# Constant rows and memory tokens made during attention, and first-stage buffers in another order, in a hybrid decoder layer

## The chip, the cores and the metric

The kernel runs on one core of a Trainium2 chip. The metric is the device time of one execution in microseconds (us), as a median over several runs. The engines are TensorE (PE, matrix products and transposes), VectorE (DVE), ScalarE (ACT), GpSimd (POOL) and SyncE (SP), which issues the transfers (DMAs). Each engine works through its own list of instructions in order and waits where an operand or a buffer is not ready yet.

## The reference, cut to what matters

One layer of a decoder on 1024 tokens of width 1024, all in float32. In the first sub-layer one input projection gives q, k, v of an attention, z, x, B, C and dt of a Mamba-2 mixer (SSD) and two gates; the second attends to 256 memory tokens; the third is a feed-forward.

```python
h = rms_norm(x, g_pre_mix[l])
q, k, v, z, xbc, dt_raw, ga, gs = _split(h @ w_in[l], IN_SIZES)
o_att = stick_breaking_attention(q, k, v)          # 16 heads
o_ssm = ssd_branch(z, xbc, dt_raw, ...)            # 32 heads in 4 groups, chunks of 128 tokens
merged = sigmoid(ga) * (o_att @ w_br_att[l]) + sigmoid(gs) * (o_ssm @ w_br_ssm[l])
x = x + rms_norm(merged @ w_mix_out[l], g_post_mix[l])
h = rms_norm(x, g_pre_xa[l])
mem_n = rms_norm(mem, g_mem[l])                    # 256 x 1024
x = x + rms_norm(memory_cross_attention(h, mem_n, w_xq[l], w_xkv[l], w_xo[l]), g_post_xa[l])
h = rms_norm(x, g_pre_ffn[l])
x = x + rms_norm(swiglu(h, w_gu[l], w_down[l]), g_post_ffn[l])
```

The mixer's decay between two tokens of a chunk is exp(a_cs[t] − a_cs[s]) for s ≤ t, and zero above the diagonal.

## The kernel before

Every float32 matrix is split into a high and a low part of a reduced format (`hi_sb`, an ACT copy on L96 or a POOL one on L92; `lo_of`, a subtraction on L99), and every product is three matmuls (L102 to L104, L213 to L215, L453 to L455). An operand must therefore be loaded, split on ACT, then on DVE, before PE can use it.

The work runs in stages. Each stage opens pools of SBUF and PSUM buffers and closes them at its end; a pool of a later stage is laid over the addresses of closed ones, and a new tile waits for the last reader of each old tile that it covers. So the order in which pools are opened decides who waits for whom. Inside a stage the build's scheduler sets the order of the instructions on every engine from its own timeline, and the code adds a few fixed orders: `behind(marks)` places what it holds after the given instructions.

1. First stage. x is loaded, normalised with the gain `g_pre_mix` (with `junk` as scratch) and transposed. The products with w_in are made in seven block products in place of eight (Strassen's way), for which sums and differences of the blocks of h and of the weights are needed: `hb` holds b11, b21, b22, t1 and later t2, t3, t4, each as high and low part (h and l at the end of the name). Here v's first products (`pv`, weights split into `vh` and `vl` of the pool vsplit) and dt (`pdt`) are made.
2. Second stage (L419 on). `rest_of_v` makes v's remaining products and then z. It begins with `s1 = a21 + a22` of weights (tile `zo`, L463), two differences (L466, L467), splits of these into `zh` and `zl` (L96, L99), and the product `mb`. t3 and t4 come back from `tc_d` in DRAM and are split.
3. Convolutions of x, B and C, dt's chain, the early gates.
4. Attention. `dense` projects q and k for two heads at a time in two PSUM buffers `mm`; the evacuation (L786 to L797) writes `qs`, `kh` and, through `gt`, `kl`, and SyncE copies halves between them. `va` and `vb` are loaded, added and split by POOL. Then scores (`sc`), a running sum on DVE (L845), transposes (`tr`), weights `wth` and `wtl`, and values (`av`); the last gates (`gt`, from `g_proj`'s dense) run between them.
5. SSD, mixed with the memory's K and V projection. The exponents of the decays are made by PE: `colrows` times `keyrows` (L1032) sums, for each pair of tokens, rows loaded from `sum_d` and `key_d` into constant patterns. These patterns are built at the stage's start (L964 to L981: POOL's selects, DVE's casts). `open_four` loads B and C of four chunks (`bfm`, `cfm`, `btm`), `prep` x (`xs`). `memory(m)` loads 128 memory tokens, normalises and transposes them and splits them into `mh` and `mlo` (tiles oth and otl).
6. The branches' outputs, the mix, cross-attention and the feed-forward.

Of the kernel before, what the change touches and what calls it, by code (L numbers as in the profile page):

```python
# [34 lines left out]
def hybrid_block(ctx, tc, a, out, dbg=None):  # L35
# [41 lines left out]
    tc_d = [scr(f"tc_d{i}", [P, 4, HALF]) for i in range(2)]  # L77
    kT_d = scr("kT_d", [P, KT, ML])
# [161 lines left out]

    HB = ("b11", "b21", "b22", "t1")
    HT = ("t2", "t3", "t4")
    LATE_GATES = 4
    with ExitStack() as pa:
# [22 lines left out]
        with ExitStack() as p1:  # L267
            t4 = pool(p1, "t4x0", 4)
            tt = pool(p1, "tcomb", 6)
            bt = pool(p1, "b12t", 3)  # L270
            vh = pool(p1, "vsplit", 8)
            mp = pool(p1, "memp")
            mt4 = pool(p1, "t4mem", 2)
# [9 lines left out]
            gx = load_gain(mp, "g_pre_mix")  # L283
# [30 lines left out]
            def normed(c, eng):  # L314
                xt = xts[c]
                junk = mk(mt4, [P, D], BF16, "junk")
# [82 lines left out]
            d11, d0, d1 = [mk(mt4, [64, HALF], F32, "du", bufs=3) for _ in range(3)]  # L399
# [320 lines left out]
        with ExitStack() as p2:  # L720
# [84 lines left out]

            def gate_proj(gi):
                def ev(ps, half):
                    gt = mk(t2, [P, HALF], F32, "gt")
                    A.activation(gt, ps, AF.Sigmoid)
# [95 lines left out]
            for q in qk_quanta(0):  # L905
                for f in q:
                    f()
            NM = 2 * NH
# [15 lines left out]


# [8 lines left out]
    with ExitStack() as p3:  # L934
        AHEAD = 2
        gb = pool(p3, "gbs", 2)
# [3 lines left out]
        ep = pool(p3, "exps", 1)  # L940
# [15 lines left out]

        NROW, HEADS, ONES, PAIRS, LARGE = 2, 32, 0, 64, 2.0 ** 127
# [5 lines left out]
        before, within = mk(t4, [P, GH, P], F32, "s4"), mk(t4, [P, GH, P], F32, "s4")  # L968
        G.memset(before, 1.0)
        G.affine_select(before, before, [[0, GH], [-1, P]], ALU.is_gt, 0.0, base=-2 * PAIRS, channel_multiplier=2)  # L970
        within = within[:, 0:4]
        G.memset(within, -(2.0 ** 120))
        G.affine_select(within, within, [[0, 4], [1, P]], ALU.is_ge, 0.0, base=2 * PAIRS, channel_multiplier=-2)
        G.affine_select(within, within, [[0, 4], [-1, P]], ALU.is_ge, 0.0, base=1 - 2 * PAIRS, channel_multiplier=2)
        hr = slice(HEADS, HEADS + 2 * GH)
        for t in colrows:
            V.tensor_copy(t, before)
            V.tensor_tensor(t[hr], *[ident[hr, HEADS + j * GH:HEADS + (j + 1) * GH].unsqueeze(2).to_broadcast([2 * GH, GH, P]) for j in range(2)], ALU.add)
        for t in keyrows:
            V.tensor_copy(t.rearrange("p (c s) -> p c s", s=P), within)  # L980
            V.tensor_scalar(t[ONES:ONES + 2], low[ONES:ONES + 2, 0:1].to_broadcast([2, HALF]), 0.0, 1.0, ALU.mult, ALU.add)  # L981
# [84 lines left out]
        def outp(n):  # L1066
# [30 lines left out]
        def flip(n):  # L1097
# [8 lines left out]
            for k in range(4):  # L1106
                T.transpose(pt[:, k, :], y[:, k * P:(k + 1) * P], ident)
# [41 lines left out]
        gj = mk(wp, [P, 4, D], F32, "bw")  # L1149
        gm, junk_m = gj[:, 0], gj[:, 1]  # L1150
        marks = []

        def memory(m):
            xt = mk(wr, [P, D], F32, "wraw")
            nc.sync.dma_start(xt, a["mem"][0][m * P:(m + 1) * P, :])
            ms = mk(stats, [P, 1], F32, "ms")
            A.activation(junk_m, xt, AF.Square, scale=D ** -0.5, accum_out=ms)
            V.scalar_tensor_tensor(xt, xt, rstd_of(ms), gm, ALU.mult, ALU.mult)
            for kh in range(2):
# [695 lines left out]
```

## Time and profile before

| what | value |
|---|---|
| median of 3 runs | 2599.42 us (2596.26 to 2602.25) |
| the profiled execution | 2601.74 us, its span 2600.0 us |
| PE busy | 2494.5 us, 96% of the span |
| DVE, ACT, POOL busy | 69%, 44%, 33% |
| HBM read and written | 199.84 MB and 74.19 MB |

The span is what the profile covers; the run's own time is 1.74 us longer. PE's share is high nearly all the way: in the page's 40 slices of 65 us only the first shows less than 80%. Waits of PE are thus short and lie at the joints of stages. In rows of a timeline the first number is the start, the second the busy time, "xN" the count of instructions drawn together, and the bracket the idle time of the engine just before and what ended it.

### The profile page before, as it was taken

Reading aid. Unit: us, or ns where it says so; the run is one execution under the profiler, and the core shown is the slowest. Engines: PE = TensorE matmul, PEld = TensorE weight load, DVE = VectorE, ACT = ScalarE, POOL = GpSimd, SP = SyncE. Lnnn points to the kernel's source line nnn. Section 1 sums busy time; section 2 is a strip of 40 time slices with the busy share of each in tenths; the row PEclk is TensorE's granted clock in tenths of the full one; section 3 lists DMA queues with packets and bytes.
Section 4 is the critical chain, followed back from the end, with each engine's and each line's share of the span. In section 5 each row is a group of like instructions: output and inputs, shape, how many; then the busy total and the mean of one; then the engine's idle time right before and its main releaser. Section 6 shows DMA issues by size and latency. Waiting matters only on the chain. (4 is left out here: it accounts for less than half of the span.)

```text
span 2600.0 us, 32345 instructions
## 1 busy us (share of the span) xinstructions
PE 2494.5 (96%) x11866; PEld 2061.7 (79%) x11866; DVE 1805.3 (69%) x2091; ACT 1135.6 (44%) x2023; POOL 849.8 (33%) x652
## 2 busy tenths in 40 slices
PE   6999999999999999989999999999999999999998
PEld 5788787787887878877888788887787888887877
DVE  6656868767587887587788665415459666665997
ACT  5233455555455665555544312314333333334343
POOL 3221543443111211254555150101114323323662
PEclk9999999999999999999999999999999999999999
DMA  7331432332543434355332472311232232224232
GB/s 252 136 98 56 147 130 87 114 106 89 155 102 101 110 102 106 90 177 186 108 93 70 143 251 85 121 58 49 82 117 73 77 97 74 85 94 162 98 130 97
DMA packets 254983, 292.92 MB, mean 113 GB/s; under 512 B 16991, under 2 KB 175208, under 8 KB 254698
## 3 DMA queue, kind: packets, MB, share of 16 engines
q1 hardware_dynamic: 254826, 290.87, 35.7%
q8 instruction: 93, 1.52, 0.2%
q14 instruction: 64, 0.52, 0.1%
HBM read 199.84 MB, written 74.19 MB: 105 GB/s over the span
## 5 line engine op out<-in xcount | busy, mean ns | idle before, releaser
L845 DVE TENSOR_TENSOR_SCAN n<-n,mask 128x128 f32<-128x128 f32 (+7 forms) x128 | 188.6, 1499 | 23.5 <-ACT n L844 22.2
L99 DVE TENSOR_TENSOR sw<-sf,sw 128x512 fp32r<-128x512 f32 x150 | 131.0, 885 | 66.5 <-ACT sw L96 66.2
L181 POOL TENSOR_TENSOR sf<-wr,wr 128x512 f32<-128x512 f32 x38 | 59.1, 1554 | 275.9 <-DMA wr<-in_w_gu_dram 139.9
L862 ACT ACTIVATE wth<-tr,mone 128x512 fp32r<-128x512 f32 x192 | 110.4, 584 | 83.2 <-PE tr L859 82.3
L96 ACT ACTIVATE sw<-sf 128x512 fp32r<-128x512 f32 x150 | 91.9, 627 | 110.8 <-PE mm L215 94.1
L863 DVE SCALAR_TENSOR_TENSOR wtl<-tr,wth 128x512 fp32r<-128x512 f32 x192 | 99.7, 544 | 51.5 <-ACT wth L862 51.4
L96 ACT ACTIVATE sw<-wr 128x512 fp32r<-128x512 f32 x113 | 71.0, 629 | 128.9 <-PE mm L215 128.7
L102 PE MATMUL mm<-oth,bw 128*128 128x512 f32 (+1 forms) x320 | 122.6, 383 | 4.7 <-DVE a L1144 2.4
L215 PE MATMUL mm<-h,sw 128*128 128x512 f32 x320 | 125.0, 392 | 1.8 <-DVE sw L99 1.8
L213 PE MATMUL mm<-h,sw 128*128 128x512 f32 x320 | 123.0, 392 | 2.9 <-ACT h L96 2.3
L214 PE MATMUL mm<-h,sw 128*128 128x512 f32 x320 | 125.3, 392 | 0.0
L104 PE MATMUL mm<-oth,bw 128*128 128x512 f32 (+1 forms) x320 | 119.5, 374 | 1.4 <-DVE bw L99 1.4
L99 DVE TENSOR_TENSOR sw<-wr,sw 128x512 fp32r<-128x512 f32 x113 | 102.1, 904 | 25.8 <-ACT sw L96 17.8
L103 PE MATMUL mm<-otl,bw 128*128 128x512 f32 (+1 forms) x320 | 119.0, 372 | 0.0
L598 DVE SCALAR_TENSOR_TENSOR b<-b,prmT,b 128x1023 f32<-128x1023 f32 (+2 forms) x72 | 106.1, 1474 | 12.1 <-ACT b L596 11.5
L92 POOL TENSOR_SCALAR v<-va 128x512 fp32r<-128x512 f32 x16 | 20.6, 1287 | 286.4 <-PE av L872 166.7
L844 ACT ACTIVATE n<-sc 128x512 f32<-128x512 f32 (+1 forms) x192 | 88.5, 493 | 45.7 <-PE tr L859 28.9
L150 POOL TENSOR_SCALAR rstd<-ms 128x1 f32<-128x1 f32 x74 | 27.5, 372 | 231.2 <-ACT x L1366 111.0
L102 PE MATMUL p<-bw,h 128*128 128x512 f32 x256 | 99.0, 392 | 3.3 <-DVE x L1368 2.4
L104 PE MATMUL p<-bw,h 128*128 128x512 f32 x256 | 100.2, 392 | 0.0
L103 PE MATMUL p<-bw,h 128*128 128x512 f32 x256 | 99.9, 390 | 0.0
L183 POOL TENSOR_TENSOR sf<-wr 128x512 f32<-128x512 f32 x38 | 62.4, 1641 | 112.1 <-DVE sw L99 112.1
(608 smaller groups left out, 8069.6 us busy)
## 6 DMA issues: line engine op xcount, KB each, us to landing
wr<-in_w_gu_dram SPq DMA_DIRECT2D x80, 256.0 KB
wr<-in_w_in_dram SPq DMA_DIRECT2D x36, 512.0 KB
zr<-in_w_in_dram SPq DMA_DIRECT2D x28, 512.0 KB
gu_d<-t SPq DMA_DIRECT2D x44, 256.0 KB
wraw<-in_w_in_dram SPq DMA_DIRECT2D x20, 512.0 KB
zs_d<-zo SPq DMA_DIRECT2D x32, 256.0 KB
xs_d<-b SPq DMA_DIRECT2D x32, 256.0 KB
kl<-gt SPq DMA_DIRECT2D x64, 128.0 KB
```

Source lines behind the costliest of these rows:

```text
L96: A.activation(o, i, AF.Copy)
L99: eng.tensor_tensor(o, i, hi.bitcast(F32), ALU.subtract)
L102: first = T.matmul(ps, sh, mh, start=start, stop=False)
L103: T.matmul(ps, sh, ml, start=False, stop=False)
L104: T.matmul(ps, sl, mh, start=False, stop=stop)
L213: T.matmul(ps, w[0][:, k, :], bh, start=first and k == 0, stop=False, skip_group_check=True)
L214: T.matmul(ps, w[0][:, k, :], bl, start=False, stop=False, skip_group_check=True)
L215: T.matmul(ps, w[1][:, k, :], bh, start=False, stop=last and k == 3, skip_group_check=True)
L598: V.scalar_tensor_tensor(acc[:, sh:], y[:, :S - sh], cw(3 - sh, f), acc[:, sh:], ALU.mult, ALU.add)
L845: V.tensor_tensor_scan(nt[:, 0:L][:, ::-1], nt[:, 0:L][:, ::-1], mask[:, S - L:][:, ::-1], 1.0, ALU.mult, ALU.max)
L862: A.activation(wh[:, t0 * P:], pt[:, t0 * P:], AF.Identity, bias=mone)
L863: V.scalar_tensor_tensor(wl[:, t0 * P:], pt[:, t0 * P:], -1.0, wh[:, t0 * P:].bitcast(F32), ALU.add, ALU.subtract)
```

## The change

Five edits, which the diff shows:

- `patterns()` and `memory()` run in the attention stage, behind the first and the second part of the first two heads' q and k projection. The patterns are made once and stored to DRAM (`colpat_d`, `keypat_d`); the two tiles of memory tokens are normalised, transposed, split and stored to `mem_d`. The SSD stage loads them: colrows twice, keyrows twice, mh and mlo in two halves each.
- The pool `ep`, which holds low, colrows and keyrows, is opened first in the SSD stage, and so lies over other old tiles (b22 and its neighbours) than before.
- A small activation `warm` behind the last gate brings in the exponential's table.
- `flip(n)`'s transposes are placed behind the last diagonal matmul of chunk n + 2.
- The first stage's pools are opened in another order, two of them new (`dtu` for the tiles du, `gain`), one renamed (`sqs`, the junk).

```diff
+    colpat_d = scr("colpat_d", [P, S])
+    keypat_d = scr("keypat_d", [P, HALF])
+    mem_d = [scr(f"mem_d{i}", [P, KT, ML]) for i in range(2)]
...
         with ExitStack() as p1:
+            vh = pool(p1, "vsplit", 8)
+            bt = pool(p1, "b12t", 3)
+            dp = pool(p1, "dtu", 3)
+            mp = pool(p1, "memp")
+            gp = pool(p1, "gain")
+            jp = pool(p1, "sqs", 2)
             t4 = pool(p1, "t4x0", 4)
             tt = pool(p1, "tcomb", 6)
-            bt = pool(p1, "b12t", 3)
-            vh = pool(p1, "vsplit", 8)
-            mp = pool(p1, "memp")
-            mt4 = pool(p1, "t4mem", 2)
...
+                    gated.append(A.activation(gt, ps, AF.Sigmoid))
...
+            def patterns():
+                col, row, t = [mk(bp, [P, S], F32, "n1") for _ in range(3)]
+                before = t.rearrange("p (h s) -> p h s", s=P)
+                G.memset(before, 1.0)
+                G.affine_select(before, before, [[0, GH], [-1, P]], ALU.is_gt, 0.0, base=-2 * PAIRS, channel_multiplier=2)
+                V.tensor_copy(col.bitcast(F32R), t)
...
+                V.tensor_tensor(col[hr].rearrange("p (h s) -> p h s", s=P).bitcast(F32R), *heads, ALU.add)
+                nc.sync.dma_start(colpat_d, col)
...
+            def memory():
+                gm = mk(bp, [P, S], F32, "n1")
+                junk = mk(bp, [P, HALF], F32, "n0").bitcast(BF16)
+                nc.sync.dma_start(gm, a["g_mem"][0].partition_broadcast(P))
+                for m in range(2):
+                    xt = mk(bp, [P, S], F32, "n1")
+                    nc.sync.dma_start(xt, a["mem"][0][m * P:(m + 1) * P, :])
+                    ms = mk(stats, [P, 1], F32, "ms")
+                    A.activation(junk, xt, AF.Square, scale=D ** -0.5, accum_out=ms)
+                    V.scalar_tensor_tensor(xt, xt, rstd_of(ms), gm, ALU.mult, ALU.mult)
+                    for kh in range(2):
+                        pt = mk(pst, [P, HALF], F32, "tr")
+                        for k in range(4):
+                            T.transpose(pt[:, k * P:(k + 1) * P], xt[:, (kh * 4 + k) * P:(kh * 4 + k + 1) * P], ident)
+                        hi, lo = [mk(wt, [P, HALF], F32R, "wt" + n) for n in "hl"]
+                        A.activation(hi, pt, AF.Copy)
+                        V.tensor_tensor(lo, pt, hi.bitcast(F32), ALU.subtract)
+                        for d, t in zip(mem_d, (hi, lo)):
+                            nc.sync.dma_start(d[:, kh * 4:kh * 4 + 4, m * P:(m + 1) * P], t.bitcast(F32).rearrange("p (k t) -> p k t", t=P))
+
+            for n, q in enumerate(qk_quanta(0)):
                 for f in q:
                     f()
+                if n == 0:
+                    patterns()
+                if n == 1:
+                    memory()
...
+            with behind(gated[-1:]):
+                A.activation(warm, mone, AF.Exp)
...
+        ep = pool(p3, "exps", 1)
         gb = pool(p3, "gbs", 2)
...
-        ep = pool(p3, "exps", 1)
...
         for t in colrows:
-            V.tensor_copy(t, before)
-            V.tensor_tensor(t[hr], *[ident[hr, HEADS + j * GH:HEADS + (j + 1) * GH].unsqueeze(2).to_broadcast([2 * GH, GH, P]) for j in range(2)], ALU.add)
+            nc.sync.dma_start(t.rearrange("p h s -> p (h s)").bitcast(F32), colpat_d)
         for t in keyrows:
-            V.tensor_copy(t.rearrange("p (c s) -> p c s", s=P), within)
-            V.tensor_scalar(t[ONES:ONES + 2], low[ONES:ONES + 2, 0:1].to_broadcast([2, HALF]), 0.0, 1.0, ALU.mult, ALU.add)
+            nc.sync.dma_start(t.bitcast(F32), keypat_d)
...
+            d["last"] = ins
...
-            for k in range(4):
-                T.transpose(pt[:, k, :], y[:, k * P:(k + 1) * P], ident)
+            with behind([chk[n + 2]["last"]] if n + 2 in chk else []):
+                for k in range(4):
+                    T.transpose(pt[:, k, :], y[:, k * P:(k + 1) * P], ident)
...
-        with behind(chk[AHEAD - 1]["issued"]):
-            nc.sync.dma_start(gm, a["g_mem"][0].partition_broadcast(P))
-            for m in range(2):
-                memory(m)
+        for kh in range(2):
+            for t, src in zip((mh, mlo), mem_d):
+                nc.sync.dma_start(t[:, kh * 4:kh * 4 + 4].bitcast(F32), src[:, kh * 4:kh * 4 + 4])
```

How the instructions stand at three places, before and after. First DVE at the joint of the first and second stage (tc are block combinations of h, b22 and t2 its split blocks, zr weights, zo their sum). Before:

```order
L345 TENSOR_TENSOR tc_501<-tr_494,b_122_505 128x512
L337 TENSOR_TENSOR b22l_119<-tr_494,b22h_118 128x4x128
L348 TENSOR_TENSOR tc_500<-tr_494,tc_499 128x512
L350 TENSOR_TENSOR tc_502<-tr_484,tc_500 128x512
L337 TENSOR_TENSOR t2l_126<-tc_500,t2h_125 128x4x128
L463 TENSOR_TENSOR zo_660<-zr_371,zr_375 128x1024
L463 TENSOR_TENSOR zo_661<-zr_373,zr_377 128x1024
L466 TENSOR_TENSOR zr_371<-zr_622,zr_371 128x1024
L407 TENSOR_TENSOR du_582<-du_580,pv_602 64x512
L466 TENSOR_TENSOR zr_373<-zr_624,zr_373 128x1024
```

And after, in the same place:

```order
L359 TENSOR_TENSOR tc_511<-tr_504,b_122_515 128x512
L477 TENSOR_TENSOR zo_672<-zr_381,zr_385 128x1024
L477 TENSOR_TENSOR zo_673<-zr_383,zr_387 128x1024
L351 TENSOR_TENSOR b22l_123<-tr_504,b22h_122 128x4x128
L362 TENSOR_TENSOR tc_510<-tr_504,tc_509 128x512
L480 TENSOR_TENSOR zr_381<-zr_632,zr_381 128x1024
L480 TENSOR_TENSOR zr_383<-zr_634,zr_383 128x1024
L364 TENSOR_TENSOR tc_512<-tr_494,tc_510 128x512
L351 TENSOR_TENSOR t2l_130<-tc_510,t2h_129 128x4x128
L481 TENSOR_TENSOR zr_632<-zo_672,zr_632 128x1024
L481 TENSOR_TENSOR zr_634<-zo_673,zr_634 128x1024
L103 TENSOR_TENSOR zl_681<-zo_672,zh_680 128x512
```

The sums of weights (before L463, now L477) moved ahead of b22l and of t2l; the differences follow between them. The tile zo lies at the addresses of vl before, and of g_pre_mix and junk now.

Next DVE while q and k of the first heads are projected (mm is the projection's PSUM tile, wlo the next weights' low part, the n_ tiles those of patterns and memory). Before, behind the first evacuation of q, it reads:

```order
L788 TENSOR_TENSOR gt_5296<-mm_5269,qs_5294 128x512
L99 TENSOR_TENSOR wlo_5416<-wraw_5413,whi_5415 128x1024
L788 TENSOR_TENSOR gt_5327<-mm_5302,qs_5294 128x512
L797 TENSOR_TENSOR gt_5368<-mm_5339,kh_5364 128x512
L99 TENSOR_TENSOR wlo_5601<-wraw_5598,whi_5600 128x1024
```

After:

```order
L802 TENSOR_TENSOR gt_5308<-mm_5281,qs_5306 128x512
L927 CAST n_871_5314<-n_873_5316 128x1024
L930 TENSOR_TENSOR n_871_5314<-ident_91 16x1024
L103 TENSOR_TENSOR wlo_5505<-wraw_5502,whi_5504 128x1024
L802 TENSOR_TENSOR gt_5353<-mm_5328,qs_5306 128x512
L936 CAST n_872_5315<-n_872_5315 128x512
L937 TENSOR_SCALAR n_872_5315<-ident_91 2x512
L950 SCALAR_TENSOR_TENSOR n_881_5368<-n_881_5368,rstd_5372,n_879_5365 128x1024
L811 TENSOR_TENSOR gt_5457<-mm_5428,kh_5453 128x512
```

The pattern's cast and addition stand in front of the weights' split and the second q half, the memory's first norm in front of the first k half.

Last, SyncE at the SSD's start (g_d is a late gate's store, o_d attention's output). Before:

```order
L991 DMA bfm_9976<-bf_d 128x512
L993 DMA cfm_9978<-cf_d 128x512
L810 DMA g_d<-gt_9900 128x512
L995 DMA btm_9980<-bt_d_64 128x4x128
L995 DMA btm_10392<-bt_d_64 128x4x128
L877 DMA o_d_70<-oT_9893 64x512
L877 DMA o_d_71<-oT_9893 64x512
L989 DMA keyrows_2051_9954<-key_d 8x512 x2
L1025 DMA colrows_2049_9952<-sum_d 1x8x128 x2
L1025 DMA colrows_2050_9953<-sum_d 1x8x128 x2
L1239 DMA bw_9973<-in_g_mem_dram 128x1024
L1155 DMA wraw_10034<-in_mem_dram 128x1024
```

After:

```order
L1025 DMA colrows_2072_10042<-colpat_d 128x1024
L1025 DMA colrows_2073_10043<-colpat_d 128x1024
L826 DMA g_d<-gt_9989 128x512
L1027 DMA keyrows_2074_10044<-keypat_d 128x512
L1027 DMA keyrows_2075_10045<-keypat_d 128x512
L1037 DMA bfm_10054<-bf_d 128x512
L1039 DMA cfm_10056<-cf_d 128x512
L1041 DMA btm_10058<-bt_d_64 128x4x128
L1071 DMA colrows_2072_10042<-sum_d 1x8x128 x2
L1071 DMA colrows_2073_10043<-sum_d 1x8x128
L1035 DMA keyrows_2074_10044<-key_d 8x512
```

Four loads of patterns stand ahead of bfm, cfm and btm, and the rows of sum_d and key_d are written into the loaded tiles; the loads of xs, which stood before all of these, now come behind them.

More of the change, by code (lines that the diff above doesn't have):

```diff
@@ L1148, in hybrid_block @@
         mlo = mk(ot, [P, KT, ML], F32R, "otl")
-        gj = mk(wp, [P, 4, D], F32, "bw")
-        gm, junk_m = gj[:, 0], gj[:, 1]
         marks = []
[L1153 to L1159, printed above, removed]
-                pt = mk(ps, [P, 4, P], F32, "mm", bufs=2)
-                for k in range(4):
-                    T.transpose(pt[:, k, :], xt[:, (kh * 4 + k) * P:(kh * 4 + k + 1) * P], ident)
-                ks, cs = slice(kh * 4, kh * 4 + 4), slice(m * P, (m + 1) * P)
-                A.activation(mh[:, ks, cs], pt, AF.Copy)
-                V.tensor_tensor(mlo[:, ks, cs], pt, mh[:, ks, cs].bitcast(F32), ALU.subtract)
         def mem_quanta():
```

28 lines of the change are left out of this document (14 added, 14 removed).

## The prediction

> **What bounds the kernel now.** I read the page's first two parts, then the windows around the three places that the change touches, then the timelines of single engines inside them.
>
> ```profile
> span 2600.0 us, 32345 instructions
> PE 2494.5 (96%) x11866; PEld 2061.7 (79%) x11866; DVE 1805.3 (69%) x2091; ACT 1135.6 (44%) x2023; POOL 849.8 (33%) x652
> ```
>
> PE is busy for 2494.5 of 2600.0 us, so at most 105.5 us can be won by removing its waits, plus whatever its clock loses. A change that leaves the matrix work alone, as this one nearly does, is worth what it does to those 105 us. The windows (columns: stretch, length, then busy time and count of PE, weight load, DVE, ACT, POOL; granted clock, DMA share, GB/s) say where some of them lie:
>
> ```profile
> 56.00:58.00 2.00, 1.97 (x9) 0.91 (x7) 2.00 (x2) 0.60 (x1) 0.00 (x0) 1.00 0.17 67
> 58.00:64.00 6.00, 0.00 (x0) 0.00 (x0) 5.87 (x7) 1.70 (x4) 2.09 (x2) 0.71 0.56 141
> 64.00:76.00 12.00, 9.05 (x24) 6.71 (x25) 12.00 (x14) 7.52 (x14) 4.42 (x2) 0.57 0.56 183
> 76.00:100.00 24.00, 24.00 (x108) 19.87 (x107) 11.05 (x18) 4.42 (x7) 0.00 (x0) 1.00 0.41 126
> 660.00:680.00 20.00, 20.00 (x90) 16.57 (x89) 3.30 (x4) 6.57 (x10) 8.50 (x6) 1.00 0.82 242
> 680.00:700.00 20.00, 19.54 (x96) 15.89 (x95) 11.98 (x14) 10.57 (x21) 1.06 (x1) 1.00 0.49 124
> 1100.00:1140.00 40.00, 27.22 (x136) 19.75 (x135) 37.83 (x47) 26.08 (x45) 17.14 (x15) 0.91 0.57 174
> 1140.00:1240.00 100.00, 92.78 (x556) 80.17 (x555) 74.29 (x82) 55.83 (x101) 47.84 (x45) 0.98 0.56 175
> ```
>
> Three different situations. At 58 to 64 PE does nothing at all, and from 64 to 76 it runs 24 matmuls in 12 us, while right after it runs 108 in 24 us: this is where the first stage hands over to the second. At 660 to 700, where attention's first q and k are projected, PE has 0.46 us of idle time in 40, and DVE and ACT are mostly free. At 1100 to 1140, where the SSD starts, PE idles 12.8 us and DVE is busy 37.83 of 40: DVE bounds that stretch. From 1140 on PE loses another 7.2 us in 100.
>
> **The hand-over at 58 us (first-stage pools in another order).** The rows, DVE and SyncE first, then PE:
>
> ```profile
> 40.92 0.94 SPq L260 DMA_DIRECT2D zr<-in_w_in_dram  x1
> 44.69 0.69 DVE L345 TENSOR_TENSOR tc<-tr,b 128x512 f32<-128x512 f32 x1 [0.33 <-PE tr L325]
> 46.32 0.69 DVE L337 TENSOR_TENSOR b22l<-tr,b22h 128x512 fp32r<-128x512 f32 x1 [0.94 <-ACT b22h L336]
> 48.31 0.69 DVE L337 TENSOR_TENSOR t2l<-tc,t2h 128x512 fp32r<-128x512 f32 x1
> 55.94 2.36 DVE L463 TENSOR_TENSOR zo<-zr,zr 128x1024 f32<-128x1024 f32 x2 [6.94 <-PE pv L214]
> 58.22 1.22 DVE L466 TENSOR_TENSOR zr<-zr,zr 128x1024 f32<-128x1024 f32 x1
> 59.95 1.21 DVE L466 TENSOR_TENSOR zr<-zr,zr 128x1024 f32<-128x1024 f32 x1
> 61.09 2.34 DVE L467 TENSOR_TENSOR zr<-zo,zr 128x1024 f32<-128x1024 f32 x2
> 66.13 4.64 DVE L99 TENSOR_TENSOR zl<-zo,zh 128x512 fp32r<-128x512 f32 x4
> 57.58 0.39 PE L396 MATMUL pdt<-b21l,wds 128*64 128x512 f32 x1
> 64.10 2.08 PE L453 MATMUL mb<-zh,t1h 128*128 128x512 f32 x4 [6.13 <-ACT zh L96]
> 69.02 0.80 PE L454 MATMUL mb<-zl,t1h 128*128 128x512 f32 x1 [2.85 <-DVE zl L99]
> ```
>
> The next product needs zh and zl, the halves of zo, the sum of L463. DVE is free from 49.0 us (48.31 + 0.69), but L463 does not start until 55.94: its operands are weights, and what releases it is a PE matmul of the old product pv. That is a wait for memory, not for data: zo lies where vl lay, which the last v matmuls read. Then everything queues on DVE, ACT splits at 64, PE gets its first four matmuls at 64.10 and the next at 69.02. With the pools in the other order zo, zh and zl lie over the gain row, the junk of the norm and the x tiles, last read by the first stage's transposes, the last of which releases L345; the order has L463 right behind L345. So from 45.4: two L463 to 47.7, b22l to 48.4, one combination (0.69) to 49.1, two L466 (2.4) to 51.5, a combination and t2l (1.4) to 52.9, L467 to 55.3, four zl at about 0.65 each, as the short ones of this form are here, from 55.3 to 57.9. PE finishes its last pdt at 58.0, starts with the four zh matmuls, and by then has all its zl. The cover for the DVE sums is thus PE's own work to 58 us, with nothing to spare at the end but nothing missing either; b22l and t2l come 1.4 and 4 us later than before.
>
> The price: 24 matmuls of this kind take 24 x 24.00/108 = 5.3 us in the next window; now they take the 18 us from 58 to 76. That is 12.7 us. I take 12.5, since the first zl may be late by a few tenths. Upper end 13; lower end 8, if the weights a11, whose load is issued at 40.92, arrive some us late for L466 and push the zl back. The half-clock belongs to this sum: the granted clock is 0.71 and 0.57 in the two windows and 1.00 on both sides, so it goes with the gap. The Trainium skill, "TensorE: Matmul & The Clock Gate", Part 1 (the HAM clock gate), says the clock halves after an idle window of about 3.4 us and returns after about as much sustained work. The trace agrees in kind: the gap is 6 us, and by that rule a leftover gap below 3.4 us would cost only itself.
>
> What is late next: the t3 and t4 splits are not needed until the later products, and PE then runs without a gap for 24 us. The first-stage sums stand ahead of them, not behind.
>
> **The SSD start (rows and tokens loaded instead of made).**
>
> ```profile
> 1086.01 2.36 POOL L970 TENSOR_SCALAR_AFFINE_SELECT s<-s 128x1024 f32<-128x1024 f32 x1
> 1090.67 1.45 DVE L99 TENSOR_TENSOR s2r<-s,s2r 128x512 fp32r<-128x512 f32 x1 [2.15 <-ACT s2r L96]
> 1097.67 0.42 SPq L993 DMA_DIRECT2D cfm<-cf_d  x1
> 1101.79 0.63 ACT L96 ACTIVATE ch<-cfm 128x512 fp32r<-128x512 f32 x1 [2.01 <-DMA cfm<-cf_d]
> 1104.65 1.29 DVE L977 CAST colrows<-s 128x1024 fp32r<-128x1024 f32 x2
> 1105.85 0.76 DVE L980 CAST keyrows<-s 128x512 fp32r<-128x512 f32 x2
> 1106.64 2.35 DVE L978 TENSOR_TENSOR colrows<-ident 16x1024 fp32r<-16x1024 f32 x2
> 1110.56 0.70 PE L1032 MATMUL dec<-colrows,keyrows 128*128 128x512 f32 x2 [0.36 <-DMA colrows<-sum_d]
> 1131.41 1.43 PE L1162 MATMUL mm<-ident,wraw 128*128 128x128 f32 x8 [3.32 <-DVE otl L1165]
> L1158 DVE SCALAR_TENSOR_TENSOR wraw<-wraw,rstd,bw 128x1024 f32<-128x1024 f32 x2 | 3.6, 1776 | 0.2 <-POOL rstd L151 0.2
> L1165 DVE TENSOR_TENSOR otl<-mm,oth 128x512 fp32r<-128x512 f32 x3 | 2.0, 677 | 0.0
> ```
>
> Removed from DVE: 1.29 + 0.76 + 2.35 + 3.6 + 2.0 = 10.0 us of the 37.83, all where DVE is the bound; with them go PE's wait of 3.32 us for otl and its 16 transposes. Given back: in the new order the s2r splits that stood ahead (1090.67 is one) come into this stretch, some 2 to 3 us. The warm table load adds nothing in sum; it only moves up.
>
> What replaces it is DMA, ordered by memory again: colrows and keyrows now lie over b22, which the last late-gate matmuls read, so their loads are issued at about 1097, with cfm. They are 1.5 MB, with bfm, cfm and btm 2.3 MB; the window moves 174 GB/s at a share of 0.57, so 305 GB/s full, 7.5 us: landed about 1105. Then sum_d's rows are written into colrows, a second DMA in series. cfm shows what a lone one takes, 1097.67 to 1101.79, 4.1 us; so the first exponent matmul comes at 1109 to 1110, against 1110.56 now. Nothing is gained up to there; the gain comes after it, from the lighter DVE, at most 10 us less the 2.5 given back. The memory halves are another 2 MB (6.6 us at that rate) in the queue with the first weights, and PE's projection of K could use them from about 1117. I take 4 us, half of 7.5, since xs and weights share the queue with 2 MB that were not there. Ends: +10 and −3. The Trainium skill, "DMA: Bandwidth & Descriptors", Anatomy of one DMA, gives about 2.0 us fixed a DMA, most of it the receipt of the last write, and would speak against a copy through DRAM followed by a dependent write. By its figures the series takes an estimated 5.2 us plus the queue, no worse than mine, and the 4.1 us of cfm contain it.
>
> **The projection of q and k (patterns and memory added).** Here the change adds work where PE has no slack:
>
> ```profile
> 658.24 1.03 PE L588 MATMUL tr<-ident,b 128*128 128x128 f32 x8
> 659.09 0.50 PE L102 MATMUL mm<-b11h,whi 128*128 128x512 f32 x1
> 664.53 2.40 POOL L822 TENSOR_TENSOR va<-va,vb 128x1024 f32<-128x1024 f32 x1 [6.57 <-DMA vb<-v_d]
> 672.39 0.69 DVE L788 TENSOR_TENSOR gt<-mm,qs 128x512 fp32r<-128x512 f32 x1
> 675.74 0.60 ACT L795 ACTIVATE kh<-mm 128x512 fp32r<-128x512 f32 x1 [3.38 <-PE mm L104]
> 678.92 3.30 SPq L779 DMA_DIRECT2D kl<-gt  x4
> 683.70 0.56 PE L842 MATMUL sc<-kh,qs 128*128 128x128 f32 x3
> ```
>
> Sixteen transposes at 1.03/8 cost 2.1 us by their busy time, 1.7 us by the pace at which eight of them pass (658.24 to 659.09): I take 1.7 lost in full, since PE is busy 20.00 of 20. The DVE work is half of 1.29, 0.76 and 2.35 (one copy of each now), the norms' 3.6 and four differences at 0.677: 8.5 us; DVE has 24.7 us free in these 40, so it costs nothing by its sum. These steps cost by their place in the queues. POOL: a memset and a select (the 2.36 of L970) behind va at 664.53 and in front of the v splits. DVE: the cast waits for POOL, and the split of the next weights and gt (before at 672.39) are queued behind it. ACT: the Square of memory tile 0 stands in front of kh's evacuation (before at 675.74) and waits for a load, whose buffer is the one that the cast reads; k's second half needs kh's PSUM buffer. SyncE: the store of the pattern waits for DVE, and memory tile 0 waits for its buffer; the q copies, two weight loads and keypat are behind them; the kl copies come 1 to 2 us later. PE's first scores at 683.70 are the consumer. The walk: va ends at 666.9, memset, select and a gap put the pattern at about 671.5; the cast ends at 672.2, the load, at cfm's 4.1 us, at 676.3, so the Square ends near 677.5 and kh comes 1.5 to 3 us later; two PSUM buffers cover most. Between 0 and 5 us of stall, I take 1: the row it is nearest to is the window's 0.46 us of idle. If that cover is gone (a load landing 5 us later than I think), every us of it is one of PE.
>
> Flip's transposes behind a later pd move four short matmuls on PE, 0 ± 1 us.
>
> **Sum.** 12.5 + 4 − 1.7 − 1 = 13.8 us. From the profiled execution (span 2600.0, run 2601.74) that is about 2588; from the median of 2599.42 it is 2585.6. A measurement of this kernel tells 0.2%, 5.2 us, from no change.
>
> **Rivals.**
>
> 1. The SSD start gains nothing, or attention stalls by its full 5 us: DMA takes DVE's place as bound. For it: DMA is at 0.57 on average there and about 3.5 MB come into 20 us. Against: PE waited mostly for DVE, not DMA. Gain 12.5 + 0 − 1.7 and − 1 to − 5, so 6 to 10: 2590 to 2594, with the −3 2597. Chance 0.18.
> 2. The SSD start recovers nearly all, +10, and attention hides everything: 12.7 + 10 − 1.7 = 21, 2578. For it: 20 us of idle to win there. Against: the loads start no earlier than 1097. Chance 0.13.
> 3. The gap at 58 us is only renamed: L463 goes early, but L466 or zl waits for something else (the a11 load, or a PSUM bank), so DVE finishes where it did. For it: the chain on DVE has no slack at 57.9. Against: DVE idle 6.94 us in the row above, with its data there. Gain about 2: 2595 to 2600. Chance 0.06.
> 4. Slower. The added steps block attention's queues: ACT's Square stands in order in front of kh, and kh in front of all scores. If memory tile 0 lands at 676 it costs 1 us; each us later is one. It decides against the change only when it eats 13.8 and 5.2 more beyond that 1 us, a landing at 695. For it: the load waits for the cast, the cast for POOL, POOL for va, and the DMA share of 0.82 at 660 to 680 is the highest window here. Against: va ends at 666.9, memset and select take under 4 us, and 512 KB at 242 GB/s take 2.2 us. Time 2605 to 2615. Chance 0.05.
>
> **How the numbers follow.** The forecast itself (2580 to 2590) has 0.58. Faster by over 0.2% is below 2594.2: forecast, rival 2 and most of rival 1, 0.58 + 0.13 + 0.16 = 0.87. Within 0.2%: rival 3 and the rest of rival 1, 0.08. Slower 0.05. The range runs from below rival 2, with the scatter of the median (±3), to rival 1's middle: 2575 to 2594.
>
> **What would show it.** In the new trace: L463's successor starts near 45.5 without a wait for PE; the windows 58 to 76 have the clock 1.00 and PE full; zl's first use waits under 1 us. At 660 to 690 there are 16 more transposes, and PE waits under 2 us for kh or PSUM. At the SSD start the first exponent matmul comes at the same distance from the last value matmul, DVE is busy 27 to 31 of 40 us, and no wait of 3 us for otl. I am wrong if the gap of 58 us reappears under another releaser, if PE shows a wait of over 5 us in the q and k projection, or if exponent matmuls wait for colrows by more than 3 us.

## The result and the profile after

The changed kernel takes 2596.68 us, the median of 12 runs (2594.89 to 2607.05), against 2598.78 us for the kernel before, beside it (12 runs). The ratio is 0.9994, with a 95% interval of 0.9985 to 1.0003: no change that can be told. The forecast was 2585.6 us with a range of 2575 to 2594, so it was wrong, by some 11 us. The profiled execution spans 2594.7 us, against 2600.0; the profiled run of before lay some 2 to 3 us above its own median, and the medians differ by 2.1 us, which the interval doesn't tell from nothing.

The windows of the changed kernel, asked for the same stretches (columns as in the prediction), and one more at 640:

```profile
58.00:64.00 6.00, 6.00 (x29) 4.92 (x28) 2.03 (x4) 0.59 (x1) 6.00 (x3) 1.00 0.32 80
64.00:76.00 12.00, 12.00 (x54) 9.76 (x53) 5.39 (x9) 5.88 (x11) 0.50 (x2) 1.00 0.67 215
640.00:660.00 20.00, 16.77 (x70) 13.31 (x70) 2.93 (x5) 7.02 (x10) 6.43 (x5) 0.91 0.54 170
660.00:680.00 20.00, 17.10 (x80) 13.62 (x78) 8.78 (x8) 5.63 (x9) 10.84 (x11) 1.00 0.95 265
680.00:700.00 20.00, 19.51 (x94) 16.29 (x94) 17.25 (x19) 13.09 (x29) 1.82 (x3) 0.91 0.77 217
1100.00:1140.00 40.00, 33.14 (x188) 27.43 (x187) 26.41 (x32) 21.49 (x37) 15.92 (x13) 0.87 0.89 278
1140.00:1240.00 100.00, 91.67 (x534) 78.25 (x534) 84.98 (x92) 59.35 (x108) 55.08 (x50) 1.00 0.55 175
```

The gap at 58 us is gone, as forecast: PE is full and its clock is 1.00. From 640 to 700 PE now lacks 6.6 of 60 us, at a DMA share that went to 0.95; before it lacked 3.4 (two of its windows are in the prediction, this is the third):

```profile
640.00:660.00 20.00, 17.03 (x80) 13.69 (x81) 13.37 (x12) 8.61 (x14) 7.01 (x4) 1.00 0.44 128
```

At the SSD's start PE does 33 us of work in 40 where it did 27.

So the expected gain was made and then lost again. Where, is seen by following PE's lead: for every matmul that both kernels have, its start in the trace of before less its start in the other trace; the table gives the median over the 20 us of the time of before that begin at the number in its head. A positive number is time won up to there. The first column is behind the hand-over, 600 ahead of the convolutions' end, 660 at q's first matmuls, 740 behind the first heads, 1080 at attention's end, 1260 and 1440 inside the SSD, 2560 near the end.

| kernel | 120 | 600 | 660 | 740 | 1080 | 1260 | 1440 | 2560 | median us, ratio to before |
|---|---|---|---|---|---|---|---|---|---|
| changed kernel | 11.7 | 13.6 | 8.9 | −0.1 | 1.3 | 8.8 | 5.2 | 5.5 | 2596.68, 0.9994 (0.9985 to 1.0003) |
| pools_only | 12.3 | 13.4 | 8.6 | 8.6 | 8.6 | 3.8 | 3.2 | 5.5 | 2598.98, 1.0000 (0.9989 to 1.0011) |
| all_but_pools | 0.9 | 2.7 | 2.8 | −3.5 | −2.7 | 0.9 | 0.8 | −1.6 | 2604.59, 1.0017 (1.0007 to 1.0028) |
| pools_tail_pinned | 11.7 | 13.3 | 12.7 | 12.6 | 11.9 | 5.3 | 5.3 | 8.8 | 2594.63, 0.9983 (0.9974 to 0.9993) |
| square_behind_k | 11.2 | 13.2 | 9.2 | 0.4 | 2.7 | 6.6 | 5.3 | 6.8 | 2597.71, 0.9990 (0.9980 to 1.0000) |
| patterns_only | 11.5 | 13.2 | 8.4 | 5.2 | 7.0 | 2.2 | 1.9 | 4.7 | 2598.07, 0.9995 (0.9985 to 1.0004) |
| memory_only | 8.3 | 8.3 | 2.3 | −4.9 | −3.7 | −1.7 | −2.4 | −3.1 | 2601.75, 1.0001 (0.9992 to 1.0011) |
| flip_free | 12.0 | 13.8 | 7.9 | 0.9 | 3.8 | 6.7 | 6.1 | 9.2 | 2596.25, 0.9993 (0.9982 to 1.0004) |
| spread_and_pinned | 11.4 | 11.1 | 10.6 | 11.0 | −7.4 | −3.7 | −6.8 | −7.1 | 2609.19, 1.0037 (1.0024 to 1.0051) |
| pools_tail_flip | 9.5 | 11.4 | 9.3 | 9.1 | 9.6 | 6.2 | 6.1 | 6.0 | 2592.42, 0.9972 (0.9962 to 0.9981) |
| all_tail_pinned | 11.8 | 13.2 | 12.7 | 5.6 | 7.0 | 11.5 | 11.1 | 11.2 | 2590.75, 0.9970 (0.9961 to 0.9980) |
| all_tail_flip_early | 11.8 | 13.4 | 12.9 | 7.1 | 8.1 | 12.6 | 12.3 | 13.1 | 2594.02, 0.9976 (0.9966 to 0.9986) |
| traffic_alone | 11.0 | 12.6 | 12.0 | 9.5 | 10.5 | 10.4 | 10.4 | 9.9 | 2591.68, 0.9971 (0.9961 to 0.9982) |

Each lead is of one execution, counted against the one profile of before, and single executions of one kernel differ by up to 13.7 us in all (flip_free, 2592.55 to 2606.22). A step of the lead inside one row is read more safely than its end, but it scatters too. Up to 1080 us the changed kernel and flip_free have the same order of instructions on every engine and of the transfers (by line, tile name and shape), and from 660 to 740 they lose 9.0 and 7.0 us. From 1085 to 1255 the changed kernel and all_tail_pinned have the same orders, and from 1080 to 1260 they win 7.5 and 4.5 us. So a difference of 2 to 3 us between two steps is not told from scatter. The medians come from 5 to 12 runs, each ratio from runs of both kernels on the same chip.

In the first row there are three losses: 4.8 us between 600 and 660, 9.0 between 660 and 740, 3.6 behind 1260. The first two in the rows of the changed kernel, PE, DVE and ACT:

```profile
644.11 1.51 PE L602 MATMUL tr<-ident,b 128*128 128x128 f32 x8 [2.54 <-POOL b L614]
650.24 0.50 PE L106 MATMUL mm<-b11h,whi 128*128 128x512 f32 x1 [0.69 <-ACT b L633]
661.71 1.78 DVE L927 CAST n<-n 128x1024 fp32r<-128x1024 f32 x1 [3.77 <-POOL n L926]
663.52 2.19 DVE L930 TENSOR_TENSOR n<-ident 16x1024 fp32r<-16x1024 f32 x1
667.96 0.50 PE L106 MATMUL mm<-t1h,whi 128*128 128x512 f32 x1 [1.11 <-DVE gt L802]
668.15 1.06 ACT L949 ACTIVATE n<-n 128x1024 bf16<-128x1024 f32 x1 [4.64 <-DMA n<-in_mem_dram]
678.96 1.06 ACT L949 ACTIVATE n<-n 128x1024 bf16<-128x1024 f32 x1 [8.43 <-DMA n<-in_mem_dram]
679.79 0.68 PE L858 MATMUL sc<-kh,qs 128*128 128x128 f32 x3 [1.80 <-DMA kh<-kh]
684.21 1.71 PE L954 MATMUL tr<-ident,n 128*128 128x128 f32 x8
```

At 644.11 PE waits for POOL's product of the last convolution tile. In the kernel before, these eight transposes (there L588, at 658.24, with no wait) stand behind the last twelve matmuls of their stage; now they stand in front of them. The wait is 2.54 us, then the clock drops (0.91 in that window; eight transposes take 1.51 us instead of 1.03), then ACT's evacuation is 0.69 us late. With the 1.8 us that a clock of 0.91 takes from 20 us these are 5.0 us, about the 4.8 lost. Nothing in the change touches this place. The engines' orders are dealt by the scheduler from its own timeline, and that had shifted.

### The profile page after: what moved, and what is told of

The parts are those of the page before. It is cut to its first block, busy times and chain, and to the rows that moved or that the text cites. A ratio compares the mean times of both kernels' runs of the same rounds, so it can differ in the third digit from the quotient of the medians.

```text
span 2594.7 us, 32373 instructions
## 1 busy us (share of the span) xinstructions
PE 2494.0 (96%) x11866; PEld 2058.7 (79%) x11866; DVE 1798.7 (69%) x2087; ACT 1133.1 (44%) x2024; POOL 855.3 (33%) x652
## 5 line engine op out<-in xcount | busy, mean ns | idle before, releaser
L612 DVE SCALAR_TENSOR_TENSOR b<-b,prmT,b 128x1023 f32<-128x1023 f32 (+2 forms) x72 | 105.1, 1460 | 11.8 <-ACT b L610 11.3
```

The lines of the kernel that those rows point to most:

```text
L612: V.scalar_tensor_tensor(acc[:, sh:], y[:, :S - sh], cw(3 - sh, f), acc[:, sh:], ALU.mult, ALU.add)
```

## The experiments

**The pools alone, and everything else alone.** pools_only is the kernel before with the changed opening order of the first stage's pools:

```diff
+            vh = pool(p1, "vsplit", 8)
+            bt = pool(p1, "b12t", 3)
+            dp = pool(p1, "dtu", 3)
...
-            bt = pool(p1, "b12t", 3)
-            vh = pool(p1, "vsplit", 8)
```

> Only the first stage's pools in the new order; patterns, memory, SSD as before. Theory A (each part keeps its own price: the hand-over wins 11.7 to 13.6 us, the last convolution transposes, moved ahead by the shifted timeline, cost 4.8 us, the added steps in the q and k projection cost the other 9): PE is 13.6 us ahead at 640 us, 8.8 us ahead from q's projection on and stays so: about 2590. Rival B (attention cannot use PE's lead, since its loads or its copies arrive when they arrive): the lead shrinks to 0 to 2 us within attention although nothing was added there: about 2597.

all_but_pools is the changed kernel with that edit undone.

> The whole change without the new pool order. Theory A: no gain at the hand-over, no 4.8 us at the convolution's end, 9 us lost in the q and k projection, 7.5 won at the SSD's start, 4 to 6 lost again in the SSD: about 2604 to 2607, slower than before. Rival B: the q and k projection loses only its 1.7 to 3 us, since the rest was the lead being given up: 2597 to 2600.

Theory A held in kind up to attention's end: pools_only is 13.4 us ahead at 600, loses the same 4.8 us at the convolutions' end, and then keeps 8.6 us through all of attention. all_but_pools keeps the old order at the convolutions' end and loses nothing there; it loses 6.3 us in q's and k's projection. So the two losses belong to different edits, and rival B is out, though the second came out at 6.3 us and not at 9. But neither theory foresaw what came next: pools_only, whose SSD is the old one, loses 4.8 us at the SSD's start, and its median is that of the kernel before.

**The convolutions' end.** pools_tail_pinned adds to pools_only a fixed place for the eight transposes (`done` holds the stage's last matmul):

```diff
+                        with behind(pin):
                             T.transpose(pt[:, c * P:(c + 1) * P], acc[:, cc * P:(cc + 1) * P], ident)
...
-                    tail(*pend.pop(0))
+                    tail(*pend.pop(0), done if c0 == order[-1][0] and len(pend) == 0 else ())
```

> pools_only, and the eight transposes of the last convolution tile are placed behind the last matmul of their stage, where they stand in the kernel before. Theory A: the wait of 2.5 us for POOL's product and the half clock behind it go; PE is 13 us ahead also in the q projection: about 2586. Rival: the place of these transposes does not matter, PE waits for the same POOL product or for the evacuation instead: as pools_only, about 2590 under theory A.

The lead is 12.7 at 660 and 11.9 at 1080: 0.6 us are lost instead of 4.8, so the place of these transposes was nearly all of it in this run. pools_tail_flip, with the same orders up to here, still lost 2.1 us; in both kernels PE waits 2.44 us for ACT at 633 to 634, and only in pools_tail_flip is the clock low behind it (0.83 from 630 to 640, against 1.00). all_tail_pinned is the same edit on the changed kernel.

> The whole change, with the last convolution transposes pinned as in pools_tail_pinned. If the parts keep their prices: PE is 4 to 5 us further ahead at 660 and at 1080 us than in the changed kernel (about 5.5 at 1080), about 2592. If the lead is again used up in the q and k projection, where transfers bound it: 1 to 2 us ahead at 1080, 2596.

It reaches 2590.75 us, ratio 0.9970 (0.9961 to 0.9980): with one order fixed in a stage that the change does not touch, the median lies 5.9 us lower, and the interval is clear of no change. It is the best of the kernels tried, together with traffic_alone and pools_tail_flip, from which it can't be told apart. These two make patterns and memory in the SSD as before, so no run shows that moving them gains anything in the total.

**Who takes the 9 us in q's and k's projection.** square_behind_k puts ACT's Squares behind k's last evacuation:

```diff
+                    with behind(kev[-1:]):
                         A.activation(junk, xt, AF.Square, scale=D ** -0.5, accum_out=ms)
```

> The whole change, with the memory tokens' two Squares on ACT placed behind the last evacuation of k's first projection. Theory A says the Squares' waits of 4.6 and 8.4 us for their loads hold up k's evacuation and with it the first scores: without that the q and k projection loses 3 to 5 us instead of 9: about 2591 to 2594. Rival C: the 16 transposes, the pattern's cast in front of gt, and the DMA queue are the loss: no change, 2596 to 2598.

The loss from 660 to 740 is 8.8 us, as before: rival C. My blame on the Squares, in the prediction and in this expectation, was wrong, although the profile shows them waiting 4.6 and 8.4 us in front of kh. Four of PE's waits in this kernel from 650 to 745 us (total, times, longest; a fifth, 1.8 us of av for wtl, has 1.2 us in the kernel before):

```profile
PE sc L860 <- DMA kl<-gt: 1.5, 3, 0.8
PE mm L106 <- ACT b L633: 1.5, 1, 1.5
PE mm L106 <- DVE gt L802: 1.4, 1, 1.4
PE sc L859 <- DMA kh<-kh: 1.0, 1, 1.0
```

Two of them are copies by DMA, one is gt, behind the pattern's cast and addition on DVE; the one for ACT's b is still the convolutions' end. patterns_only builds the memory tokens in the SSD as before, memory_only the patterns.

> The whole change, but the memory tokens are made in the SSD stage as before; only the patterns are made during q's and k's projection. If the patterns (their cast and addition in front of gt on DVE) are a small part of the 9 us lost there and the memory the larger: the loss from q's projection to 740 us is 2 to 3 us, PE is 5.5 to 7 us ahead at 1080 us. If the patterns are the larger part: the loss is 6 or more. Total 2594 to 2600, since the SSD's order is dealt anew.

> The whole change, but the patterns are built in the SSD stage as before; only the memory tokens are made during q's and k's projection. If the memory's 3.5 MB of transfers and 16 transposes are the larger part: the loss from q's projection to 740 us is 5 to 7 us, PE is 1.5 to 3.5 us ahead at 1080 us. If it was the patterns: a loss of 2 to 3 us. Total 2594 to 2600.

patterns_only loses 3.2 us from 660 to 740, memory_only 7.2: the memory is the larger part. In patterns_only PE waits 1.2 us for gt and 1.1 for the copies:

```profile
PE mm L106 <- DVE gt L802: 1.2, 1, 1.2
PE sc L858 <- DMA kh<-kh: 0.9, 1, 0.9
PE sc L859 <- DMA kl<-gt: 0.2, 1, 0.2
```

traffic_alone adds to pools_tail_pinned 4 MB of copies that nothing reads, two behind each group of q's and k's copies, and no work on any other engine:

```diff
+            for e in range(4):
+                with behind([evs[e]]):
+                    for i in range(2):
+                        nc.sync.dma_start(spare_d[2 * e + i], w_in[(2 * e + i) * P:(2 * e + i + 1) * P, 0:S])
```

> pools_tail_pinned (no patterns and no memory tokens in attention) with eight added copies of 512 KB from DRAM to DRAM, 4 MB, about what patterns and memory move, two behind each of the four copies of q's and k's projection on SyncE; nothing reads them. It adds transfers there and no work on PE, ACT, DVE or POOL. If crowded transfers are what the added steps pay for in the q and k projection: PE loses 3 to 6 us from 660 to 740 us (pools_tail_pinned loses 0.1 there, the changed kernel 9, of which 1.7 to 2 are transposes). If it is the place of their instructions on ACT, DVE and POOL: under 1 us lost.

It fills the transfers as the changed kernel does, 0.99 of the 16 engines (first row, traffic_alone; second, pools_tail_pinned):

```profile
660.00:680.00 20.00, 20.00 (x93) 16.65 (x92) 6.79 (x10) 5.42 (x11) 3.45 (x2) 1.00 0.99 306
```

```profile
660.00:680.00 20.00, 20.00 (x96) 16.69 (x95) 7.36 (x10) 5.88 (x12) 3.45 (x2) 1.00 0.70 192
```

It loses 2.5 us from 660 to 740, between the two expectations; 0.9 us of that are waits for copies, and PE's order there was dealt partly anew. As an estimate, of the 9 us about 2.5 go with the transfers, about 1.7 to 2 are the transposes, and 0.9 to 2.0 are gt behind the cast (PE's wait for it in five kernels). What is left, some 3 us, isn't assigned further; part of it is a lower clock (0.91 from 680 to 700, 1.8 us in 20). These parts come from different executions, which scatter by 2 us here. The prediction's 2.7 us held the transposes and about a seventh of the rest.

spread_and_pinned is all_tail_pinned with patterns and memory tiles made at steps 4, 8 and 12 of attention, one at a time (with the Square's scratch in a buffer n1 in place of n0).

```diff
+                if m in STEPS:
+                    [patterns, lambda: memory([0]), lambda: memory([1])][STEPS.index(m)]()
```

> The whole change with the last convolution transposes pinned as in pools_tail_pinned, and with patterns and the two memory tiles made one at a time in the middle of attention (steps 4, 8 and 12 of 32), where the DMA share is below 0.4 instead of 0.9 to 1.1. If crowding at 660 to 690 us is what the added steps pay for: PE is 9 to 11 us ahead at 1080 us (13.3 less 0.6, 1.7 of transposes and about 1), about 2588 to 2592. If the steps cost the same anywhere, by their place in the engines' queues: 3 to 5 us ahead, about 2594.

It missed both expectations: the three steps cost 3, 9 and 8 us (20 in all, of which 2 come back by 1080), where the transfers are lighter (0.47 and 0.48 of the engines from 740 to 800 and to 860). Its waits of PE from 740 to 860 us name another resource:

```profile
PE av L890 <- ACT wth L881: 6.5, 2, 3.3
PE tr L878 <- DVE wtl L960: 2.8, 2, 2.1
```

wtl of L960 is the memory's own low part, and wth and wtl are the four buffers that attention's values go through. In mid attention the memory takes buffers that every step needs; at its start, where the change puts it, they are not yet in use. That these buffers alone are the cause was not tried.

**The SSD.** Why does pools_only lose 4.8 us where its code is the old one, and pools_tail_pinned 6.6? Both traces show the same waits, which the kernel before does not have; here those of pools_tail_pinned:

```profile
1119.66 1.12 PE L1112 MATMUL ptr<-ident,s 128*128 128x128 f32 x4 [2.86 <-ACT s L1099]
1135.13 1.11 PE L1112 MATMUL ptr<-ident,s 128*128 128x128 f32 x4 [4.69 <-ACT s L1099]
```

These are flip's transposes. PE's order of the diagonal products (p, one per chunk) and the flips (F) says why:

```
before              p p p F p F p F p F p F
pools_only          p p F p F p p F p F p F
pools_tail_pinned   p p F p F p p F p F p F
traffic_alone       p p p F p F p F p F p F
changed kernel      p p p F p F p F p F p F
```

In the two kernels that lose, the first flips stand one chunk earlier, and PE waits in order for ACT's scaled rows. traffic_alone has the same source in its SSD as pools_tail_pinned; its flips were dealt as before's, no wait for ptr of any length stands in its list, and its lead is 10.5 at 1080 and 10.4 at 1260. The same instructions, dealt in another order, lose 6.6 us or nothing. The two orders differ in more than the flips, on every engine. pools_tail_flip fixes the flips by the change's own edit (flip behind the diagonal product of chunk n + 2):

> pools_tail_pinned with flip's transposes behind the diagonal matmul of chunk n + 2; patterns and memory as before. In pools_tail_pinned PE's lead of 11.9 us at 1080 us shrinks to 5.3 at 1250 us, and PE waits 2.9 and 4.7 us for flip's operand, since the dealt order has the first flips one chunk earlier than the kernel before. If these waits are where the lead goes: 9 to 12 us of lead at 1250 us, about 2588 to 2590. If the SSD's start gives the lead up for another reason (DVE, the loads): 5 to 6 us as before, about 2594.

The waits for ptr are gone, and 3.4 us are lost instead of 6.6: about half of the loss went with the flips, the rest is spread over other waits. Early flips aren't needed for such a loss either: patterns_only, whose flips stand as before's, loses 4.8 us here. The longest of PE's waits in this kernel, 1083 to 1260 (total, times, longest), are an exponent matmul's for ACT and a projection's:

```profile
PE dec L1037 <- ACT s L1038: 3.3, 1, 3.3
PE mm L102 <- ACT wraw L1230: 2.0, 1, 2.0
```

flip_free undoes that edit in the changed kernel; all_tail_flip_early is all_tail_pinned with that edit for the first ten chunks alone.

> The whole change without the order that puts flip's transposes behind the diagonal matmul of chunk n + 2. If that order is what costs 0.4 to 1.5 us at each group of four chunks from 1250 to 1440 us (PE then waits for cb with nothing else at hand): PE's lead is the same at 1440 as at 1250 us, 3 to 4 us better at the end of the SSD: about 2593. If the SSD's dealt order is the cause: no change within 2 us, 2595 to 2598.

> all_tail_pinned, with flip's place fixed only for the first ten chunks, that is at the SSD's start. If the fixed place costs 0.4 to 1.5 us per group of chunks afterwards and is of use only at the start: 3 us less than all_tail_pinned, about 2589. If flip_free's flat lead from 1250 to 1440 us had another cause: as all_tail_pinned.

From 1080 to 1260 flip_free wins 2.9 us, the changed kernel 7.5, all_tail_pinned with the changed kernel's orders 4.5. With flip free, a wait for ptr is back:

```profile
PE ptr L1154 <- ACT s L1141: 2.4, 1, 2.4
```

From 1260 to 1440 it loses 0.6 and the changed kernel 3.6, which looks as if the fixed place cost 3 us later on. all_tail_pinned refutes that: with the same fixed place it loses 0.4 there. Nor is the 3.6 a matter of the dealt order: from 1260 us to the end the order of every engine is the same in all these traces but that of spread_and_pinned. It is one execution's own: some 1.6 us are its clock (0.96 from 1380 to 1420, where all_tail_pinned has 1.00), and the rest stays open. all_tail_flip_early tests nothing after all, because its orders came out as those of all_tail_pinned from the start to the end; its 2594.02 us against 2590.75 is what two builds with one order differed by.

## Why the prediction was wrong, point by point

- **The hand-over: right.** 12.5 us were forecast; the lead is 11.7 at 120 and 13.6 at 600. DVE's chain came out nearly as walked, L477 (before L463) first:

```profile
45.56 3.33 DVE L477 TENSOR_TENSOR zo<-zr,zr 128x1024 f32<-128x1024 f32 x2
53.48 2.35 DVE L481 TENSOR_TENSOR zr<-zo,zr 128x1024 f32<-128x1024 f32 x2
55.75 2.48 DVE L103 TENSOR_TENSOR zl<-zo,zh 128x512 fp32r<-128x512 f32 x4
58.07 0.39 PE L467 MATMUL mb<-zh,t1h 128*128 128x512 f32 x1
58.30 0.40 PE L468 MATMUL mb<-zl,t1h 128*128 128x512 f32 x1
```

  The lower end occurred too, but not by a late load of a11: in memory_only and pools_tail_flip zl came 1.8 us late and the lead was 8.3 and 9.5. All orders up to there are those of the changed kernel. What differs is who gives way, DVE or POOL. POOL of the changed kernel, then DVE and POOL of memory_only:

```profile
54.83 9.21 POOL L484 TENSOR_TENSOR zr<-zr,zr 128x1024 f32<-128x1024 f32 x2 [8.16 <-DVE zr L481]
55.81 6.86 DVE L103 TENSOR_TENSOR zl<-zo,zh 128x512 fp32r<-128x512 f32 x4
54.89 6.03 POOL L484 TENSOR_TENSOR zr<-zr,zr 128x1024 f32<-128x1024 f32 x2 [8.15 <-DVE zr L481]
```

  The four zl take 2.48 us where POOL's two subtractions take 9.21, and 6.86 where those take 6.03. The prediction had zl at 0.65 each and nothing beside them; that this came true in ten of the twelve traces with the new pools was in part luck, since their orders up to there are the same.

- **"The added steps in q's and k's projection: 1.7 and 1 us": the mis-sized term.** Measured: 9.0 us in the changed kernel, 6.3 to 8.8 in the others that have them all in this place (7.1 and 5.8 with the transposes pinned). The step that failed is "the row it is nearest to is the window's 0.46 us of idle": an idle time of a window before the change says nothing of a window with 4 MB more in it. The row that mattered was quoted beside it, DMA at 0.82 of its engines; at 0.95 to 0.99 the k copies arrive late (PE waits 1.8 us for kh in the changed kernel, 0.9 us for kh and kl in traffic_alone). The walk through the queues was also too kind: DVE's cast was begun at 661.71 after the wait for POOL, as walked, but the cast and the addition took 4 us together, where I had taken 1.8 (half of 1.29 and 2.35), and gt was 1.1 us late. No single wait came near the 5 us that the prediction named as its sign of being wrong (the longest is 1.8 us, for kh); the loss is made of many short ones. Cast and addition ran beside these of POOL:

```profile
661.64 3.00 POOL L103 TENSOR_TENSOR v<-va,v 128x512 fp32r<-128x512 f32 x2
665.17 1.05 POOL L934 TENSOR_SCALAR_AFFINE_SELECT n<-n 128x512 f32<-128x512 f32 x1
```

- **"What is late next" at the hand-over: the missing term.** The sum carried the lead through 2500 us as if the later order stood. It does not: 4.8 us went at the convolutions' end, in code that the change does not touch. The lists of the two orders show this place; I compared them only at the places that the diff names. The 3.6 us in the SSD's body are no such term, since the orders there are the same.

- **The SSD's start: right in kind and sign.** 4 us were forecast, with −3 to +10; the lead grows by 7.5, and by 3.6, 3.9 and 4.5 in all_but_pools, square_behind_k and all_tail_pinned, whose SSD has the same source. DVE is busy 26.41 of 40 us (27 to 31 forecast, so a little less), the first exponent matmul comes 4.7 us behind the last value matmul (5.8 before), and K's projection starts at 1115:

```profile
1105.14 1.78 PE L1053 MATMUL dec<-cfm,bfm 128*128 128x128 f32 x8 [2.23 <-DMA cfm<-cf_d]
1107.26 1.30 PE L1078 MATMUL dec<-colrows,keyrows 128*128 128x512 f32 x2 [0.34 <-DMA keyrows<-key_d]
1115.18 0.41 PE L106 MATMUL mm<-oth,bw 128*128 128x256 f32 x1
```

  The loads now hold up the stage's first products, as the first rival had it, at a DMA share of 0.89, but PE waits only 2.2 us for them and the gain is not lost. The Trainium skill gives its 2.0 us fixed per DMA ("DMA: Bandwidth & Descriptors", Anatomy of one DMA) for transfers issued by GpSimd; these are issued by SyncE. It did not speak against the copy through DRAM here: keyrows and colrows made PE wait 0.3 and 0.4 us. Flip's edit, priced at 0 ± 1, is probably part of this gain: flip_free wins 0.7 to 4.6 us less here than the kernels with it.

- **The chances.** The time lies within rival 3's 2595 to 2600, and just above rival 1's 2590 to 2594, by neither's mechanism: the gap was not renamed and the SSD's start did gain. That rival 3's range was met is chance. 0.08 for "within 0.2%" was too little, because no rival held a loss outside the diff.

## What to carry to other kernels

Where a scheduler deals the order, a gain early in the program is not carried to the end for nothing: compare the whole lists of before and after on the bound engine, not only the places in the diff, and follow the lead of equal instructions through two traces; a loss in untouched code can be pinned back with one order (here one line: 4.2 us of lead, and medians 5.9 and 2.7 us lower in two builds with the same orders). Before a step of such a lead is explained, see whether the orders differ there at all and how far two traces with one order lie apart (here up to 3 us in a stage). Work that is moved into a full stage is to be priced by the resource that it fills up, transfers among them, and not by the idle time that the stage had without it.

## What was not expected of the hardware

With every one of PE's matmuls unchanged and 4 MB of unrelated copies beside them, PE lost 2.5 us in 80; DVE's cast and addition took 1.78 and 2.19 us beside POOL's subtractions (1.5 us each), where the pairs before took 1.29 and 2.35 us for two, beside no work of POOL. Other runs show that this goes with POOL's work and not with the instruction, since the dealt order put other work beside it. The pair in all_tail_pinned (beside a memset and selects) and in spread_and_pinned (beside a memset, then a select):

```profile
659.03 0.98 DVE L930 CAST n<-n 128x1024 fp32r<-128x1024 f32 x1 [4.92 <-POOL n L929]
661.62 1.53 DVE L933 TENSOR_TENSOR n<-ident 16x1024 fp32r<-16x1024 f32 x1
728.98 0.68 DVE L930 CAST n<-n 128x1024 fp32r<-128x1024 f32 x1
730.10 1.22 DVE L933 TENSOR_TENSOR n<-ident 16x1024 fp32r<-16x1024 f32 x1
```

By the Trainium skill, "SBUF — State Buffer", Who interferes with whom, DVE and GpSimd share a pair of ports: a DVE instruction with two inputs in SBUF contends there with a GpSimd one that reads SBUF, and beside DVE's two-port modes whoever issues first holds the pair for the whole instruction. The 1.1 us more on the cast and 1.0 on the addition, each less than one subtraction, agree with that, and so do the zl at the hand-over, where either DVE or POOL gives way.

And at the convolutions' end a gap of 2.54 us on PE was followed by a granted clock of 0.91 over that window, while a gap of 2.44 us at 632 in the same trace left it at 1.00 (628 to 640), and gaps of 1.1 and 1.8 us at 667 and 679 stand in windows of 1.00 and 0.91. By the Trainium skill, "TensorE: Matmul & The Clock Gate", Part 1 (the HAM clock gate), an idle window is about 3.4 us long. Here shorter gaps sufficed, and their length alone does not say whether the clock falls, so the prediction's reading that a gap below 3.4 us costs only itself does not hold.
